# Hybrid decoder layer on one core: modulation weights loaded in 512-channel halves behind the input, their column sums formed on TensorE, first channel blocks without GpSimd

## Chip, cores, metric

The kernel runs on one core of a Trainium2 chip. The metric is the device time of one execution in microseconds (us): 1420.43 us is the median of three runs before the change (1417.43 to 1421.4). All numbers called a time are device time; the span of a profile is the part of it from the first to the last recorded instruction.

## What is computed

One layer of a conditioned hybrid decoder plus a final RMSNorm, for one sequence of 1024 tokens with 1024 channels. Only the start matters here:

```python
mod = silu(c) @ w_ada + b_ada        # (1, 1024) @ (1024, 6*1024)
sh1, sc1, gt1, sh2, sc2, gt2 = split(mod, 6)
h = rmsnorm(x, g_norm1) * (1 + sc1) + sh1
z = h @ w_in                         # (1024, 1024) @ (1024, 5128)
# then: gated convolution branch, mLSTM branch, merge, output projection,
# second norm with sc2/sh2, mixture of 32 experts, final RMSNorm
```

So the first product of `z` can't begin before the first rows of `sc1` and `sh1` (each 1024 long, from 8 MB of `w_ada` in all) are there for the channels that it contracts over. All inputs are float32. The products of the dense part are made of three products of rounded halves (`wh*hH + wl*hH + wh*hL`).

## The kernel before

Tokens and channels are cut in blocks of 128: 8 token blocks `xt[t]`, 8 channel blocks `xT[j]`. The program is emitted in a fixed order and each engine works through its own instructions in that order. Loads are issued on SP's queue.

**Loads (L1054 to L1075).** The first megabyte of `w_ada` (`ada_load(0)`) is issued ahead of `x`, then the 8 token blocks with the small vectors between them, then a second megabyte of `w_ada`, two half-megabyte pieces of `w_in` (`raw0`, `raw1`), and two more megabytes of `w_ada`. `run_start` then adds a third piece of `w_in` (`raw2`) and the last four megabytes. A megabyte of `w_ada` holds all 1024 rows by 256 columns: an even number is a quarter of the scale, an odd one a quarter of the shift.

**Start (`run_start`, L402).** A string lists the steps: `q` squares two token blocks on ScalarE, `r` takes their root mean square (VectorE, then GpSimd for the power), `s` scales a block, `t` transposes it with 8 products with the identity, `e` copies it back from PSUM (VectorE for blocks 0 to 2, ScalarE for the rest), `c` is `ada_chain`, `a` is `ada_cols`, `w` splits a piece of `w_in` into a rounded part `wh` (ScalarE) and the rest `wl` (GpSimd here), `v` transposes the small vectors.

**Columns of scale and shift.** `ada_chain(i)` multiplies and adds the 8 slices of a megabyte with the silu column on VectorE, 2 TENSOR_SCALAR and 6 SCALAR_TENSOR_TENSOR of 256 columns, and an addition from the third load on. `ada_cols(i)` sums over the partitions with products of 128x128 of the result by a column of ones on TensorE (8 products for loads 0 and 1, 4 for each later one).

**First products (`z_first`, L418).** Three pieces of 128 columns of `w_in` are multiplied in turn, a quarter of the contraction (2 channel blocks) at a time, so that the work can begin when the first quarter of scale and shift is known. Quarter `q` of piece `n` is the step `z` with the numbers n and q: 12 products of 128x512. `modulate(q)` forms scale and shift of 2 channel blocks, and for each block the modulated `xT[j]`, its rounded part `hH` and the rest `hL`. Blocks 0 and 6 are made on VectorE alone; the others on ScalarE (2 instructions) with the subtraction on GpSimd:

```python
"m0 w0 c2 c3 z00 a2 a3 z10 z20 m1 c4 c5 z01 a4 a5 z11 z21 m2 c6 c7 z02 a6 a7 z12 z22 m3 z03 z13 z23"
```

After it `run_late` (L457) gives up the space of `x` and `w_ada` and the rest of the dense part runs, with instructions of other parts filled in by budgets that are fixed when the program is emitted (`fill`).

Of the kernel before, what the change touches and what calls it, by code (L numbers as in the profile page):

```python
# [8 lines left out]
F32 = mybir.dt.float32  # L9
# [3 lines left out]
AF = mybir.ActivationFunctionType  # L13
OP = mybir.AluOpType
# [4 lines left out]
P = 128  # L19
T = 1024  # L20
D = 1024
NT = T // P
KT = D // P
# [19 lines left out]
def hybrid_layer_kernel(ctx: ExitStack, tc: tile.TileContext, x, c, w_ada, b_ada, g_norm1, w_in, b_if,  # L43
# [3 lines left out]
    nc = tc.nc  # L47
# [5 lines left out]
    V, S, G, PE = nc.vector, nc.scalar, nc.gpsimd, nc.tensor  # L53

    def tt(o, a, b, op, eng=V):
        return eng.tensor_tensor(out=o, in0=a, in1=b, op=op)  # L56

    def ts(o, a, s1, op0, s2=None, op1=None, eng=V):
        if op1 is None:
            return eng.tensor_scalar(out=o, in0=a, scalar1=s1, scalar2=None, op0=op0)  # L60
        return eng.tensor_scalar(out=o, in0=a, scalar1=s1, scalar2=s2, op0=op0, op1=op1)

    def stt(o, a, s, b, op0, op1):
        return V.scalar_tensor_tensor(out=o, in0=a, scalar=s, in1=b, op0=op0, op1=op1)  # L64

    def mm(o, l, r, start, stop):
        return PE.matmul(o, l, r, start=start, stop=stop)  # L67
# [15 lines left out]
    mps = ctx.enter_context(tc.tile_pool(name="mps", bufs=4, space=PSUM))  # L83
# [5 lines left out]
    hH = hTp.tile([P, KT, T], F32R, name="hH")  # L89
    hL = hTp.tile([P, KT, T], F32R, name="hL")  # L90
    st = tc.alloc_tile_pool(name="st", bufs=1, side="right")
    xall = st.tile([P, NT, D], F32, name="xall")
    xt = [xall[:, t, :] for t in range(NT)]
    xT = [xall[:, :, j * P:(j + 1) * P] for j in range(KT)]
    silc = cst.tile([P, KT], F32, name="silc")
# [3 lines left out]
    ones = cst.tile([P, P], F32, name="ones")  # L99
# [36 lines left out]
    def adab(vi, j, n):  # L136
        return vec[:, 64 + vi * KT + j:64 + vi * KT + j + n]
# [137 lines left out]
    W = Stream()  # L275
# [33 lines left out]
    araw = {}  # L309

    def ada_load(i):
        vi, q = (1, 0)[i % 2], i // 2
        araw[i] = st.tile([P, KT, 256], F32, tag="araw", bufs=8, name=f"araw{i}")
        nc.sync.dma_start(araw[i], ada_v[:, :, vi * D + q * 256:vi * D + (q + 1) * 256])

    def load_x(a, b):
        for t in range(a, b):
# [16 lines left out]

    def evacuate_x(t, ps):

        if t >= 3:
            S.copy(xt[t].rearrange("p (k n) -> p k n", n=P), ps)
        else:
            V.tensor_copy(xt[t].rearrange("p (k n) -> p k n", n=P), ps)  # L340

    pada = mps.tile([P, 512], F32, tag="m", name="pada")

    def ada_chain(i):

        a = araw[i]
        for k in range(4):
            for k0 in (0, 4):
                if k == 0:
                    ts(a[:, k0, :], a[:, k0, :], silc[:, k0:k0 + 1], OP.mult)  # L350
                else:
                    stt(a[:, k0, :], a[:, k0 + k, :], silc[:, k0 + k:k0 + k + 1], a[:, k0, :], OP.mult, OP.add)
        if i >= 2:
            tt(a[:, 0, :], a[:, 0, :], a[:, 4, :], OP.add)

    def ada_cols(i):

        vi, q = (1, 0)[i % 2], i // 2
        ks = (0,) if i >= 2 else (0, 4)
        for jj in range(2):  # L360
            o = pada[:, vi * KT + 2 * q + jj:vi * KT + 2 * q + jj + 1]
            for k0 in ks:
                mm(o, araw[i][:, k0, jj * P:(jj + 1) * P], ones[:, 0:1], k0 == 0, k0 == ks[-1])

    def tok(a):
        return a.rearrange("p (t n) -> p t n", n=P)

    def modulate(q):

        sl = slice(2 * q, 2 * q + 2)  # L370
        tt(A1[:, sl], pada[:, KT + 2 * q:KT + 2 * q + 2], adab(1, 2 * q, 2), OP.add)
        stt(A1[:, sl], A1[:, sl], 1.0, g1c[:, sl], OP.add, OP.mult)
        tt(S1[:, sl], pada[:, 2 * q:2 * q + 2], adab(0, 2 * q, 2), OP.add)
        for j in range(2 * q, 2 * q + 2):
            if j in (0, 6):
                ts(xT[j], xT[j], A1[:, j:j + 1], OP.mult, S1[:, j:j + 1], OP.add)
                V.tensor_copy(tok(hH[:, j, :]), xT[j])  # L377
            else:
                S.activation(xT[j], xT[j], AF.Identity, bias=S1[:, j:j + 1], scale=A1[:, j:j + 1])
                S.copy(tok(hH[:, j, :]), xT[j])  # L380
            tt(tok(hL[:, j, :]), xT[j], tok(hH[:, j, :].bitcast(F32)), OP.subtract, eng=V if j in (0, 6) else G)

    def load_third():

# [3 lines left out]
        nc.sync.dma_start(p["raw"], p["src"])  # L388
        W.nl += 1

    def split_on_pool(_):
        W.on_pool = 1
        W.split()

    def run_steps(steps, order_):

        for s_ in order_.split():
            steps[s_[0]](*(int(n) for n in s_[1:]))
# [1 line left out]
    psx = {}  # L400

    def run_start():  # L402
        ada_chain(0)
        run_steps({
            "q": lambda t: square_x(t, t + 2),
            "r": lambda t: rms_x(t, t + 2),
            "s": lambda t: ts(xt[t], xt[t], r1[:, t:t + 1], OP.mult),
            "t": lambda t: psx.update({t: transpose_x(t)}),
            "e": lambda t: evacuate_x(t, psx[t]),
            "c": ada_chain, "a": ada_cols, "l": ada_load, "w": split_on_pool,  # L410
            "x": lambda _: load_third(),
            "v": lambda _: vectors(),
        }, "q0 r0 s0 s1 a0 x0 l4 l5 l6 l7 t0 t1 q2 r2 e0 s2 s3 t2 q4 r4 e1 t3 s4 s5 q6 e2 t4 r6 e3 t5 s6 s7 t6 t7 "
           "c1 e4 e5 w0 w0 v0 e6 e7 a1")

    N_FIRST = 3

    def z_first(uses):  # L418

        ws = [W.take(), W.take()]  # L420
        ps2 = [zps.tile([P, 2, 512], F32, tag="z", name=f"z{i}") for i in range(2)]
        ps = [[a[:, 0, :], a[:, 1, :]] for a in ps2] + [[mps.tile([P, 512], F32, tag="m", name=f"z2_{hf}")
                                                          for hf in range(2)]]

        def third(_):
            split_on_pool(0)
            ws.append((W.pieces[2]["h"], W.pieces[2]["l"]))
            W.nu += 1

        def products(n, q):  # L430
            wh, wl = ws[n]
            for k in (2 * q, 2 * q + 1):
                for j, (a, b) in enumerate(((wh, hH), (wl, hH), (wh, hL))):
                    for hf in range(2):
                        mm(ps[n][hf], a[:, k, :], b[:, k, hf * 512:(hf + 1) * 512],
                           k == 0 and j == 0, k == KT - 1 and j == 2)

        run_steps({"m": modulate, "c": ada_chain, "a": ada_cols, "w": third, "z": products},
                  "m0 w0 c2 c3 z00 a2 a3 z10 z20 m1 c4 c5 z01 a4 a5 z11 z21 m2 c6 c7 z02 a6 a7 z12 z22 m3 z03 z13 z23")
        run_late()  # L440
        W.split()
        for i, use in enumerate(uses):
            use([ps2[i].rearrange("p a b -> p (a b)")] if i < 2 else ps[i])
        fill(3.0)
# [606 lines left out]
    n_dense = len(W.pieces)  # L1051


    ada_load(0)  # L1054

    vloads = []
    r0 = 0
# [9 lines left out]
    for t in range(NT):  # L1067
        load_x(t, t + 1)
        if t:
            for o, src in vloads[2 * t - 2:2 * t]:  # L1070
                nc.sync.dma_start(o, src)
    ada_load(1)
    W.prefetch()
    ada_load(2)
    ada_load(3)  # L1075
    run_start()
    for job in jobs:
        job()
# [1009 lines left out]
```

## Time and profile before

| | |
|---|---|
| median of 3 runs | 1420.43 us (1417.43 to 1421.4) |
| the profiled execution | 1411.8 us, span 1410.1 us |
| TensorE matmul busy | 1301.6 us (92%), 6619 instructions |
| VectorE busy | 985.6 us (70%) |
| ScalarE busy | 515.0 us (37%) |
| GpSimd busy | 318.4 us (23%) |
| first product of `z_first` starts | 37.21 us |
| the reader of its last result starts | 86.37 us |

The busy shares are means over very different stages: the dense part, in which TensorE is busy almost throughout, ends near 790 us; the experts behind it run with the transfers busy all the time. A busy TensorE is not one at its peak: the granted clock of a stretch stands beside its busy time.

### The profile page before, as it was taken

The page shows a single profiled execution, that of the slowest core. Times are in us where ns is not written, and L with a number is a line of the kernel's source. Part 1 is how long each engine was busy: PE and PEld are TensorE (multiplying, and loading weights), DVE is VectorE, ACT ScalarE, POOL GpSimd, SP SyncE. Part 2 cuts the span into 40 slices and gives each one's busy share as a digit, 9 for nine tenths or more (in the row PEclk, how much of TensorE's full clock was granted, in tenths as well). Part 3 has the DMA queues.
Part 4 walks back from the last instruction along what each step waited for, and adds up shares of the span by engine and source line. Part 5 has one row for each costly group of instructions (what it writes and reads, how often), then busy time and mean ns, then how long its engine had stood idle before and what let it go on. Part 6 is the DMA issues. An engine that isn't in the chain of part 4 may idle for free. (4 is left out here: it accounts for less than half of the span.)

```text
span 1410.1 us, 17680 instructions
## 1 busy us (share of the span) xinstructions
PE 1301.6 (92%) x6619; PEld 973.0 (69%) x6619; DVE 985.6 (70%) x1369; ACT 515.0 (37%) x685; POOL 318.4 (23%) x258
## 2 busy tenths in 40 slices
PE   4799888999999999999999599999898999999996
PEld 3677888879878888787888465656464656556743
DVE  6979998889976762556457786357576757666736
ACT  5232233323522224411232333225353444435613
POOL 2424355240421400105232101011011111111103
PEclk9799999999999999999999799999999999999998
DMA  9433433332454443354622559899999999999995
GB/s 287 134 120 135 139 132 134 116 107 78 149 172 134 145 132 111 140 183 149 199 91 75 183 224 382 325 376 410 419 411 408 406 398 405 381 404 389 396 366 228
DMA packets 121304, 337.50 MB, mean 239 GB/s; under 512 B 12532, under 2 KB 74272, under 8 KB 96384
## 3 DMA queue, kind: packets, MB, share of 16 engines
q1 hardware_dynamic: 106064, 290.81, 55.4%
q0 software_dynamic: 14672, 43.94, 8.2%
q10 hardware_dynamic: 480, 1.59, 0.3%
q8 instruction: 53, 0.87, 0.2%
q14 instruction: 35, 0.29, 0.1%
HBM read 303.37 MB, written 41.98 MB: 245 GB/s over the span
## 5 line engine op out<-in xcount | busy, mean ns | idle before, releaser
L56 DVE TENSOR_TENSOR wl<-big,wh 128x1024 fp32r<-128x1024 f32 x184 | 224.0, 1255 | 89.6 <-ACT wh L148 88.6
L148 ACT CAST wh<-big 128x1024 fp32r<-128x1024 f32 x184 | 185.6, 1049 | 152.8 <-DMA big<-in_w_e_gate_dram 80.4
L64 DVE SCALAR_TENSOR_TENSOR cacc<-u,vec,cacc 128x1024 f32<-128x1024 f32 x120 | 213.2, 1777 | 2.9
L67 PE MATMUL z<-hH,wh 128*128 128x512 f32 x512 | 167.0, 408 | 9.5 <-DVE hH L377 7.1
L67 PE MATMUL gu<-wh,tHLx 128*128 128x512 f32 x528 | 170.6, 404 | 1.6 <-ACT wh L148 1.0
L67 PE MATMUL z<-hL,wh 128*128 128x512 f32 x512 | 164.5, 403 | 0.0
L67 PE MATMUL z<-hH,wl 128*128 128x512 f32 x512 | 162.8, 399 | 0.0
L67 PE MATMUL gu<-big,tFx 128*64 128x512 f32 (+1 forms) x528 | 128.9, 625 | 0.0
L67 PEld LDWEIGHTS z<-hH,wh 128*128 128x128 f32 x512 | 97.0, 193 | 31.8 <-issue 8.2
L67 PEld LDWEIGHTS gu<-wh,tHLx 128*128 128x128 f32 x528 | 97.7, 191 | 27.5 <-ACT wh L148 6.5
L67 PEld LDWEIGHTS z<-hL,wh 128*128 128x128 f32 x512 | 98.3, 192 | 23.7
L67 PEld LDWEIGHTS z<-hH,wl 128*128 128x128 f32 x512 | 97.9, 191 | 24.2
L67 PE MATMUL gu<-wl,tHLx 128*128 128x512 f32 x264 | 106.7, 404 | 6.5 <-DVE wl L56 6.5
L1626 POOL DMA_INDIRECT y_d<-ye,idx x24 | 37.7, 1571 | 327.1 <-DVE ye L64 309.9
L56 DVE TENSOR_TENSOR wl<-raw,wh 128x1024 fp32r<-128x1024 f32 (+1 forms) x45 | 68.5, 1525 | 40.2 <-ACT wh L148 40.2
L67 PEld LDWEIGHTS gu<-big,tFx 128*64 128x64 f32 (+1 forms) x528 | 39.1, 144 | 72.3 <-issue 71.2
L56 POOL TENSOR_TENSOR acc<-acc,ar 128x1024 f32<-128x1024 f32 x24 | 72.0, 2998 | 61.0 <-ACT ar L572 52.1
L67 PE MATMUL zt<-wh,hH 128*128 128x256 f32 (+1 forms) x256 | 75.0, 293 | 2.5 <-DVE u L56 1.4
L67 PE MATMUL zt<-wl,hH 128*128 128x256 f32 (+1 forms) x256 | 73.9, 289 | 2.7 <-DVE wl L56 2.7
L67 PE MATMUL zt<-wh,hL 128*128 128x256 f32 (+1 forms) x256 | 74.1, 290 | 0.0
L67 PE MATMUL py<-wh,tHLh 128*128 128x512 f32 x256 | 72.8, 405 | 0.4 <-DVE tHLx L56 0.4
L67 PE MATMUL o<-woH,mHL 128*128 128x512 f32 x256 | 72.8, 400 | 0.0
(418 smaller groups left out, 2163.8 us busy)
## 6 DMA issues: line engine op xcount, KB each, us to landing
big<-in_w_e_gate_dram SPq DMA_DIRECT2D x64, 1024.0 KB
big<-in_w_e_up_dram SPq DMA_DIRECT2D x64, 1024.0 KB
big<-in_w_e_down_dram SPq DMA_DIRECT2D x64, 1024.0 KB
raw<-in_w_in_dram SPq DMA_DIRECT2D x38, 512.0 KB
ar<-in_w_ada_dram SPq DMA_DIRECT2D x16, 1024.0 KB
araw<-in_w_ada_dram SPq DMA_DIRECT2D x8, 1024.0 KB
y_d<-zero SPq DMA_DIRECT2D x16, 512.0 KB
xall<-in_x_dram SPq DMA_DIRECT2D x8, 512.0 KB
```

The source lines that it names most:

```text
L56: return eng.tensor_tensor(out=o, in0=a, in1=b, op=op)
L64: return V.scalar_tensor_tensor(out=o, in0=a, scalar=s, in1=b, op0=op0, op1=op1)
L67: return PE.matmul(o, l, r, start=start, stop=stop)
L148: S.copy(h, src)
L1626: G.indirect_dma_start(out=y_d[:, :], out_offset=bass.IndirectOffsetOnAxis(ap=idx[:, 1:2], axis=0), in_=src, in_offset=None, bounds_check= ...
```

## The change

Three things are altered, all within the first 90 us. The loads of `w_ada` are cut otherwise: a megabyte is now 512 columns of half of the rows, so that loads 0 to 3 give scale and shift of channels 0 to 511 and loads 4 to 7 the rest; they are issued behind all of `x` and behind the first piece of `w_in`. The sums of six of the eight loads are made on TensorE, 16 products of 128x128 by one silu column each; loads 4 and 6 still go over VectorE (4 instructions of 512 columns) and 4 products with ones. The modulation comes in two halves of 4 channel blocks; each block is scaled and shifted on VectorE, rounded on ScalarE and subtracted on VectorE. The three splits of `w_in` that ran on GpSimd run on VectorE, and the fourth token block comes back from PSUM by VectorE.

```diff
     def ada_load(i):
-        vi, q = (1, 0)[i % 2], i // 2
-        araw[i] = st.tile([P, KT, 256], F32, tag="araw", bufs=8, name=f"araw{i}")
-        nc.sync.dma_start(araw[i], ada_v[:, :, vi * D + q * 256:vi * D + (q + 1) * 256])
+
+        hq, vi, kk = i // 4, (1, 0)[i // 2 % 2], i % 2
+        araw[i] = st.tile([P, 4, 512], F32, tag="araw", bufs=8, name=f"araw{i}")
+        nc.sync.dma_start(araw[i], ada_v[:, 4 * kk:4 * kk + 4, vi * D + hq * 512:vi * D + (hq + 1) * 512])
...
-        if t >= 3:
+        if t >= 4:
             S.copy(xt[t].rearrange("p (k n) -> p k n", n=P), ps)
...
-    pada = mps.tile([P, 512], F32, tag="m", name="pada")
+    pada = [mps.tile([P, 512], F32, tag="m", name=f"pada{hq}") for hq in range(2)]
 
     def ada_chain(i):
 
-        a = araw[i]
-        for k in range(4):
-            for k0 in (0, 4):
-                if k == 0:
-                    ts(a[:, k0, :], a[:, k0, :], silc[:, k0:k0 + 1], OP.mult)
-                else:
-                    stt(a[:, k0, :], a[:, k0 + k, :], silc[:, k0 + k:k0 + k + 1], a[:, k0, :], OP.mult, OP.add)
-        if i >= 2:
-            tt(a[:, 0, :], a[:, 0, :], a[:, 4, :], OP.add)
+        a, c0 = araw[i], i % 2 * 4
+        ts(a[:, 0, :], a[:, 0, :], silc[:, c0:c0 + 1], OP.mult)
+        for k in range(1, 4):
+            stt(a[:, 0, :], a[:, k, :], silc[:, c0 + k:c0 + k + 1], a[:, 0, :], OP.mult, OP.add)
 
     def ada_cols(i):
 
-        vi, q = (1, 0)[i % 2], i // 2
-        ks = (0,) if i >= 2 else (0, 4)
-        for jj in range(2):
-            o = pada[:, vi * KT + 2 * q + jj:vi * KT + 2 * q + jj + 1]
-            for k0 in ks:
-                mm(o, araw[i][:, k0, jj * P:(jj + 1) * P], ones[:, 0:1], k0 == 0, k0 == ks[-1])
+        hq, vi, kk = i // 4, (1, 0)[i // 2 % 2], i % 2
+        for jj in range(4):
+            o = pada[hq][:, vi * 4 + jj:vi * 4 + jj + 1]
+            for k in range(1 if i in CHAINED else 4):
+                mm(o, araw[i][:, k, jj * P:(jj + 1) * P],
+                   ones[:, 0:1] if i in CHAINED else silc[:, 4 * kk + k:4 * kk + k + 1],
+                   i % 4 == 0 and jj == 0 and k == 0, i % 4 == 3 and jj == 3 and k == 3)
+
+    CHAINED = (4, 6)
...
-    def modulate(q):
-
-        sl = slice(2 * q, 2 * q + 2)
-        tt(A1[:, sl], pada[:, KT + 2 * q:KT + 2 * q + 2], adab(1, 2 * q, 2), OP.add)
+    def modulation(hq):
+
+        sl = slice(4 * hq, 4 * hq + 4)
+        tt(A1[:, sl], pada[hq][:, 4:8], adab(1, 4 * hq, 4), OP.add)
         stt(A1[:, sl], A1[:, sl], 1.0, g1c[:, sl], OP.add, OP.mult)
-        tt(S1[:, sl], pada[:, 2 * q:2 * q + 2], adab(0, 2 * q, 2), OP.add)
-        for j in range(2 * q, 2 * q + 2):
-            if j in (0, 6):
-                ts(xT[j], xT[j], A1[:, j:j + 1], OP.mult, S1[:, j:j + 1], OP.add)
-                V.tensor_copy(tok(hH[:, j, :]), xT[j])
-            else:
-                S.activation(xT[j], xT[j], AF.Identity, bias=S1[:, j:j + 1], scale=A1[:, j:j + 1])
-                S.copy(tok(hH[:, j, :]), xT[j])
-            tt(tok(hL[:, j, :]), xT[j], tok(hH[:, j, :].bitcast(F32)), OP.subtract, eng=V if j in (0, 6) else G)
+        tt(S1[:, sl], pada[hq][:, 0:4], adab(0, 4 * hq, 4), OP.add)
+
+    def modulate(j):
+
+        ts(xT[j], xT[j], A1[:, j:j + 1], OP.mult, S1[:, j:j + 1], OP.add)
+        S.copy(tok(hH[:, j, :]), xT[j])
+        tt(tok(hL[:, j, :]), xT[j], tok(hH[:, j, :].bitcast(F32)), OP.subtract)
...
     def run_start():
-        ada_chain(0)
...
-        }, "q0 r0 s0 s1 a0 x0 l4 l5 l6 l7 t0 t1 q2 r2 e0 s2 s3 t2 q4 r4 e1 t3 s4 s5 q6 e2 t4 r6 e3 t5 s6 s7 t6 t7 "
-           "c1 e4 e5 w0 w0 v0 e6 e7 a1")
+        }, "q0 r0 s0 s1 t0 t1 q2 r2 e0 s2 s3 t2 q4 r4 e1 t3 s4 s5 q6 e2 t4 r6 e3 t5 s6 s7 t6 e4 t7 e5 a0 x0 l4 l5 l6 l7 "
+           "e6 e7 v0 w0 a1 a2 a3")
...
-        run_steps({"m": modulate, "c": ada_chain, "a": ada_cols, "w": third, "z": products},
-                  "m0 w0 c2 c3 z00 a2 a3 z10 z20 m1 c4 c5 z01 a4 a5 z11 z21 m2 c6 c7 z02 a6 a7 z12 z22 m3 z03 z13 z23")
+        run_steps({"m": modulation, "h": modulate, "c": ada_chain, "a": ada_cols, "w": third, "z": products,
+                   "u": lambda _: ws.append(W.take())},
+                  "u0 m0 h0 h1 u1 z00 w0 h2 z10 h3 z20 c4 z01 z11 z21 a4 a5 c6 a6 a7 m1 h4 h5 z02 h6 z12 h7 z22 "
+                  "z03 z13 z23")
...
-    ada_load(0)
...
-    ada_load(1)
-    W.prefetch()
-    ada_load(2)
-    ada_load(3)
+    W.load()
+    for i in range(4):
+        ada_load(i)
+    W.load()
     run_start()
```

`split_on_pool`, which sent a subtraction to GpSimd, is gone; its callers now call `W.split()` itself. In the new string `m` forms scale and shift of a half, `h` modulates one channel block, and `u` takes a piece of `w_in` (for the second piece that is also its split).

## Rows read from the trace of the kernel before

**Rows 1.** The page's second part: TensorE's busy tenths and its granted clock, in 40 slices of 35 us.

```profile
PE   4799888999999999999999599999898999999996
...
PEclk9799999999999999999999799999999999999998
```

**Rows 2.** Stretches of 35 us, all engines: start and end, length, then busy time (and instructions) of PE, PEld, DVE, ACT and POOL, the granted clock of TensorE, the busy share of the DMA engines and GB/s.

```profile
105.00:140.00 35.00, 34.71 (x157) 27.91 (x156) 34.57 (x20) 9.30 (x9) 16.63 (x7) 1.00 0.36 127
...
175.00:210.00 35.00, 30.02 (x223) 29.44 (x222) 34.40 (x30) 14.67 (x17) 19.23 (x14) 0.90 0.37 120
...
1015.00:1050.00 35.00, 33.85 (x182) 22.71 (x179) 26.41 (x30) 19.13 (x23) 5.73 (x4) 1.00 1.01 416
```

**Rows 3.** The waits on TensorE from 30 to 90 us: engine, line, what was waited for, us in total, how often, the longest.

```profile
PE pada L67 <- DVE araw L56: 7.2, 4, 2.6
PE z L67 <- DVE hH L377: 7.1, 1, 7.1
```

**Rows 4.** The timeline at the first product of `z_first` and at the reader of its last one: start, us, engine, line, operation, and in brackets the idle time before it and what ended it.

```profile
37.21 1.19 PE L67 MATMUL z<-hH,wh 128*128 128x512 f32 x2 [7.14 <-DVE hH L377]
...
86.37 1.09 ACT L608 ACTIVATE sg<-z 128x512 f32<-128x512 f32 x2 [3.79 <-PE z L67]
```

**Rows 5.** Stretches of the start, columns as in rows 2.

```profile
24.00:26.50 2.50, 2.50 (x14) 2.50 (x13) 2.27 (x6) 1.09 (x2) 0.19 (x1) 0.50 1.17 297
...
27.30:29.00 1.70, 1.64 (x15) 1.40 (x14) 1.24 (x4) 1.68 (x3) 0.06 (x1) 1.00 1.11 331
...
30.10:33.70 3.60, 0.00 (x0) 0.00 (x0) 3.16 (x4) 3.54 (x4) 3.51 (x2) 1.00 1.09 345
...
34.00:40.00 6.00, 2.79 (x7) 2.24 (x8) 5.93 (x7) 1.15 (x2) 3.55 (x2) 0.50 1.12 333
...
44.60:47.20 2.60, 0.05 (x1) 0.00 (x0) 2.54 (x7) 0.00 (x0) 0.00 (x0) 0.50 1.09 347
...
61.50:64.60 3.10, 3.10 (x8) 2.43 (x8) 3.06 (x7) 3.04 (x4) 1.34 (x1) 0.50 0.00 0
...
92.00:120.00 28.00, 28.00 (x121) 22.50 (x120) 27.64 (x16) 7.50 (x8) 14.69 (x6) 1.00 0.40 132
```

**Rows 6.** The timeline where an engine stood until a load had landed: the first megabyte of `w_ada`, token blocks 4 and 7, and `raw2`; between the last two, the first product behind the last transpose.

```profile
9.22 0.61 DVE L60 TENSOR_SCALAR araw<-araw,silc 128x256 f32<-128x256 f32 x2 [6.32 <-DMA araw<-in_w_ada_dram]
...
16.57 1.06 ACT L323 ACTIVATE junk<-xall 128x1024 f32<-128x1024 f32 x1 [1.12 <-DMA xall<-in_x_dram]
...
22.02 1.06 ACT L323 ACTIVATE junk<-xall 128x1024 f32<-128x1024 f32 x1 [1.13 <-DMA xall<-in_x_dram]
...
28.90 0.27 PE L127 MATMUL pv<-ident,rows 128*128 128x128 f32 x1
...
37.66 1.04 ACT L148 CAST wh<-raw 128x1024 fp32r<-128x1024 f32 x1 [3.56 <-DMA raw<-in_w_in_dram]
```

**Rows 7.** SP's queue: its longest wait ahead of a load of `x`, and its issue of the last four loads of `w_ada`.

```profile
SPq L318 <- DMA araw<-in_w_ada_dram: 3.9, 1, 3.9
...
28.79 11.97 SPq L314 DMA_DIRECT2D araw<-in_w_ada_dram  x4
```

**Rows 8.** A stretch of 2 us in which the transfers ran short, columns as in rows 2.

```profile
12.00:14.00 2.00, 1.73 (x8) 1.64 (x8) 0.42 (x3) 1.89 (x4) 0.71 (x1) 1.00 0.49 161
```

**Rows 9.** Products of the column sums alone (tile `pada`), in two stretches; busy time of PE, PEld and DVE, then the granted clock.

```profile
11.80:13.80 2.00, 1.86 (x8) 1.78 (x8) 0.00 (x0) 1.00 0.49 165
...
29.00:30.10 1.10, 0.95 (x8) 0.97 (x8) 0.00 (x0) 1.00 1.10 350
```

**Rows 10.** Groups of instructions from 0 to 92 us: line, engine, operation, tiles, count, busy us and mean ns, idle time before them.

```profile
L64 DVE SCALAR_TENSOR_TENSOR araw<-araw,silc 128x256 f32<-128x256 f32 x48 | 21.8, 520 | 0.0
...
L60 DVE TENSOR_SCALAR araw<-araw,silc 128x256 f32<-128x256 f32 x16 | 9.2, 618 | 6.3 <-DMA araw<-in_w_ada_dram 6.3
...
L56 DVE TENSOR_TENSOR araw<-araw 128x256 f32<-128x256 f32 x6 | 6.8, 1128 | 0.2
...
L56 POOL TENSOR_TENSOR hL<-xall,hH 128x1024 fp32r<-128x1024 f32 x6 | 15.7, 2635 | 23.8 <-ACT hH L380 23.8
...
L56 POOL TENSOR_TENSOR wl<-raw,wh 128x1024 fp32r<-128x1024 f32 x3 | 7.4, 2472 | 7.0 <-ACT wh L148 7.0
...
L379 ACT ACTIVATE xall<-xall,S,A 128x1024 f32<-128x1024 f32 x6 | 7.4, 1242 | 25.2 <-DVE S L56 25.2
...
L380 ACT CAST hH<-xall 128x1024 fp32r<-128x1024 f32 x6 | 6.3, 1048 | 0.2
...
L56 DVE TENSOR_TENSOR hL<-xall,hH 128x1024 fp32r<-128x1024 f32 x2 | 2.5, 1226 | 0.1
...
L56 DVE TENSOR_TENSOR wl<-raw,wh 128x1024 fp32r<-128x1024 f32 x3 | 3.6, 1221 | 5.9 <-ACT wh L148 5.9
...
L340 DVE COPY xall<-xT 128x1024 f32<-128x1024 f32 x3 | 3.7, 1222 | 1.1 <-PE xT L332 1.1
```

**Rows 11.** The timeline, VectorE: modulation of one channel block beside no GpSimd work, and the column products of TensorE that it waited for.

```profile
71.91 0.60 PE L67 MATMUL pada<-ones,araw 128*128 128x1 f32 x4 [1.17 <-DVE araw L56]
...
73.01 0.81 DVE L61 TENSOR_SCALAR xall<-xall,A,S 128x1024 f32<-128x1024 f32 x1
```

**Rows 12.** The timeline, TensorE: two pairs of products behind one another in a stretch at half clock.

```profile
62.11 1.06 PE L67 MATMUL z<-hH,wh 128*128 128x512 f32 x2
...
62.97 1.06 PE L67 MATMUL z<-hH,wl 128*128 128x512 f32 x2
```

More of the change, by code (lines that the diff above doesn't have):

```diff
@@ L389, in load_third @@
         W.nl += 1
-    def split_on_pool(_):
-        W.on_pool = 1
-        W.split()
     def run_steps(steps, order_):
@@ L409, in run_start @@
             "e": lambda t: evacuate_x(t, psx[t]),
-            "c": ada_chain, "a": ada_cols, "l": ada_load, "w": split_on_pool,
+            "a": ada_cols, "l": ada_load, "w": lambda _: W.split(),
             "x": lambda _: load_third(),
             "v": lambda _: vectors(),
-        }, "q0 r0 s0 s1 a0 x0 l4 l5 l6 l7 t0 t1 q2 r2 e0 s2 s3 t2 q4 r4 e1 t3 s4 s5 q6 e2 t4 r6 e3 t5 s6 s7 t6 t7 "
-           "c1 e4 e5 w0 w0 v0 e6 e7 a1")
+        }, "q0 r0 s0 s1 t0 t1 q2 r2 e0 s2 s3 t2 q4 r4 e1 t3 s4 s5 q6 e2 t4 r6 e3 t5 s6 s7 t6 e4 t7 e5 a0 x0 l4 l5 l6 l7 "
+           "e6 e7 v0 w0 a1 a2 a3")
     N_FIRST = 3
     def z_first(uses):
-        ws = [W.take(), W.take()]
+        ws = []
         ps2 = [zps.tile([P, 2, 512], F32, tag="z", name=f"z{i}") for i in range(2)]
@@ L425, in third @@
         def third(_):
-            split_on_pool(0)
+            W.split()
             ws.append((W.pieces[2]["h"], W.pieces[2]["l"]))
```

## The prediction

> **What bounds the kernel now.** I read the 40 slices first. TensorE is busy for eight tenths or more from the third slice on, but for two slices where the experts begin, at nine tenths of the clock or more; the first two slices have 4 and 7 tenths, and in the second the granted clock is down to 7 [rows 1]. The change touches the first 90 us alone, so the question is by how much `z_first` ends earlier. What follows it takes a shift over: from 105 us TensorE and VectorE both run almost without a pause, later VectorE is the fuller of the two, and the experts are fed at 416 GB/s with the transfers always busy [rows 2]. All of these start from results of the dense part, in a fixed order; none has a date of its own.
>
> Next the waits and the timeline of the start. `z_first` runs from 37.2 us to 86.3 us, 49.1 us [rows 4]. Its 144 products need 144 x 0.231 = 33.3 us at full clock (28.0 us for 121 [rows 5]), so 15.8 us go elsewhere: 7.2 us to columns that wait for VectorE [rows 3], the rest to column products and half clock. VectorE is what feeds it: the chains over `w_ada` take 37.8 us there, and the additions, 1.13 us in the mean, are drawn out beside GpSimd's subtractions of 2.6 us [rows 10]. After each idle stretch TensorE runs at clock 0.50: from 34 to 40 us, and from 61.5 to 64.6 us [rows 5], where a pair of products takes 0.86 us, 0.43 each [rows 12].
>
> **The loads.** Before, a megabyte of `w_ada` lies ahead of `x`, SP waits 3.9 us for it before it can issue another token block [rows 7], and the transfers then fall to 161 GB/s [rows 8]. Block 7 lands at 22.0 us [rows 6]. Moving the megabyte behind `x` takes 1.05 MB at 345 GB/s [rows 5], 3.0 us, off that; of the wait I take 2.5 us, between 0 and 3.9, because the small vectors still stand between the blocks. Block 7 then lands at 16.5 us (15.1 to 19.0).
>
> Now all of scale and shift for half of the channels must land, not a quarter. From block 7 to the fourth `w_ada` load there are one piece of `w_in` and four megabytes, 4.72 MB, the same bytes that took 15.6 us from block 7 to `raw2` before [rows 6]. The piece at 297 GB/s takes 1.8 us; `w_ada` I price at 345 GB/s, 12.2 us, since the rows of 2 KB are nearest to the rows of 1 KB that ran at that rate [rows 5]: 14.0 us. Ends: 15.6 us, and 11.3 us at the 416 GB/s of the experts [rows 2]. The fourth load lands at 30.5 us (26.4 to 34.6). Issues on SP cost nothing: `raw2` and the last four loads are issued behind and their 12 us of issuing [rows 7] lie beside the transfers; they land some 16 us later, well ahead of their use after 54 us. [...]
>
> **Columns on TensorE.** 104 products in place of 40. Eight took 0.95 us in one stretch and 1.86 us in another [rows 9], so 16 cost 1.9 us or 3.7 us. `a1` to `a3` make TensorE wait for transfers; behind them stand only the products that need them anyway. Block 7 to the last transpose took 28.9 - 22.0 = 6.9 us [rows 6], so `a0` can begin at 23.4 us; at full clock TensorE keeps up (23.4 + 0.4 for the vectors + 4 x 1.9 = 31.4 us), and the fourth load ends last: 30.5 + 0.1 + 1.9 = 32.5 us. From column products to modulation took 0.5 us (71.91 + 0.60 to 73.01 [rows 11]): modulation begins at 33.0 us. Five PSUM tiles now share four buffers, but `z20` needs the first only after modulation has read it: nothing. Block 3's copy back on VectorE, 1.22 us [rows 10], lies ahead of block 7's last steps, and the first piece's subtraction, moved to VectorE, beside the column products: nothing.
>
> **First half.** A channel block costs 0.81 us on VectorE [rows 11], 1.05 us on ScalarE and 1.23 us on VectorE again [rows 10], with handovers (0.05 each, an estimate) 3.2 us; the subtraction waits for ScalarE and the next block's scaling is queued behind it, so blocks don't overlap. The first product starts at 33.0 + 0.81 + 1.05 + 0.15 = 35.0 us, 2.2 us earlier. Four blocks and two weight subtractions of 1.22 us [rows 10] put the last subtraction at 33.0 + 12.8 + 2.4 = 48.2 us; TensorE needs 11.1 us for its 48 products by then and waits; `z01` ends at 48.7 us. `z11` and `z21`: 24 x 0.231 = 5.6 us, to 54.3 us.
>
> **Second half.** Columns 4 to 7 are 40 products, 4.8 us, to 59.1 us. The chains `c4` and `c6` are 8 instructions in place of 70; even at twice the mean of 0.5 to 0.6 us [rows 10] they end at 52.5 and 57 us, when `a4` is due at 54.3 and `a6` at 56.7: nothing. Modulation starts at 59.6 us, `z02` at 61.6 us, and ends with block 5's subtraction at 66.0 + 0.5 = 66.5 us; blocks 6 and 7 hide behind the 60 products left, 13.9 us. End: 80.4 us. GpSimd loses 23.1 us of work and ScalarE six instructions of 1.24 us [rows 10]; nobody waits for either beyond what is counted.
>
> **The clock.** TensorE is idle or underused before 35 us and before 61.6 us. A restart costs 8 products or more at 0.43 instead of 0.23 us [rows 5, 12]; the waits for VectorE, some 2 us spare in each half, cover one of the two. I take 1.6 us for the other and 0.3 us for stragglers (0 to 5): 82.3 us instead of 86.3, **4.0 us saved**. The profiled execution took 1411.8 us with a span of 1410.1; it would take 1407.8. It lies 8.6 us under the median of the three runs, which are runs of the same program, so I take the same 4.0 us off the median: 1416.4 us.
>
> **Rivals.** About 0.3%, 4.3 us, can be told from no change.
>
> 1. *More*, 0.10: `w_ada` in rows of 2 KB comes at 416 GB/s, block 7 at 15.1 us and no restart is uncovered. That saves 4 to 9 us: 1411.8 us at best. Against it: TensorE's own columns then bind at about 31 us.
> 2. *The loads come no sooner*, 0.12: both upper ends, 34.6 us for the fourth load, 4.1 us later: the gain is gone, 1420.5 us. For it: the 15.6 us are measured; against it: the 161 GB/s show idle transfers.
> 3. *Columns at half clock*, 0.08: 23.4 + 0.4 + 4 x 3.7 = 38.6 us instead of 32.5; end 88.4 us, 1422.5 us, inside the bound. Against it: with nothing but transposes running, the clock rose from 0.50 to 1.00 [rows 5]. [...] No row shows a long run of one-column products.
> 4. *Slower*, 0.10: half clock stays from the columns through the first half. Blocks reach TensorE singly, so it is never busy for long there; 48 products at 0.43 are 20.6 us from 41.1 us on, so `z01` ends at 61.7 instead of 48.7 us, and the end at 93.4 us: 1427.5 us. It decides from the point where `z01` ends 10 us late. For it: each idle stretch before was followed by half clock [rows 5]. Against it: the pieces `z10` and `z20` are ready by then and keep TensorE busy.
> 5. *Given back later*, 0.04: VectorE is full from 92 us [rows 5], and some wait behind absorbs it: 1420.4 us.
>
> **The numbers.** The forecast has 0.56; its own range, 2 to 7 us saved, is 1413.4 to 1418.4 us, with 0.32 beyond the bound and 0.24 within. Faster: 0.32 + 0.10 = 0.42. No change: 0.24 + 0.12 + 0.08 + 0.04 = 0.48. Slower: 0.10. The range reaches from rival 1 to rival 3, 1411.8 to 1422.8 us; left out are rival 4 and the tails, under 0.2.
>
> **What the changed profile would show.** Block 7's square at 16.5 us, the last of `a3` at 32.5, the first product at 35.0, `z01` over at 48.7, 40 column products in one run up to 59 at full clock, a pause of 2.5 us, the reader of the last result at 82.3 us, and from there the same stretches 4 us earlier. No GpSimd instruction of 2.6 us before 80 us, and VectorE's subtractions all near 1.22 us. A first product after 37 us would make the loads or the columns the fault; a granted clock of 0.50 through most of 35 to 50 us would make rival 4 right.

## The result, and the profile after

The changed kernel takes 1435.93 us (median of 4 runs, 1433.2 to 1441.54), the kernel before 1418.93 us beside it (4 runs): the ratio is 1.0147, with a 95% interval of 1.012 to 1.0174. The forecast was 1416.4 us, in a range of 1411.8 to 1422.8. The time is 17 us longer by the medians, 21 us by the ratio, where 4 us less was expected.

The profiled execution took 1436.94 us with a span of 1435.1. The first thing to find is where the two kernels part. The same stretch as the second of [rows 2], put 20.6 us later, is this in the kernel after (columns as there):

```profile
195.60:230.60 35.00, 30.03 (x223) 29.44 (x222) 34.40 (x31) 14.69 (x17) 19.23 (x14) 0.90 0.38 123
```

All five engines have the same busy times as at 175 us before, to 0.02 us, with the same counts but for one instruction of VectorE (31 for 30). So by then the program does just what it did, 20.6 us late; what went wrong lies ahead of it. The rows that answer to [rows 4], the first product of `z_first` and the reader of its last one:

```profile
54.18 1.22 PE L67 MATMUL z<-hH,wh 128*128 128x512 f32 x2 [2.50 <-ACT hH L377]
...
106.96 1.09 ACT L602 ACTIVATE sg<-z 128x512 f32<-128x512 f32 x2 [3.84 <-PE z L67]
```

The first product is 17.0 us later than before (37.21) and 19.2 us later than forecast (35.0). The reader is 20.6 us later than before and 24.7 us later than forecast. Most of the loss is therefore ahead of the first product. Who is late there is in VectorE's longest wait; its timeline at the two modulations:

```profile
51.72 0.16 DVE L56 TENSOR_TENSOR A<-pada,vec 128x4 f32<-128x4 f32 x1 [18.73 <-PE pada L67]
...
52.19 0.81 DVE L61 TENSOR_SCALAR xall<-xall,A,S 128x1024 f32<-128x1024 f32 x1
```

VectorE stands 18.7 us for the column sums. That wait replaces the ones of [rows 3], in which TensorE stood for VectorE. And TensorE isn't waiting for a load in that time. Its own timeline, from the last transposes to the first product, and then the two long loads of the second half:

```profile
27.12 3.76 PE L67 MATMUL pada<-silc,araw 128*128 128x1 f32 x32
...
31.19 20.48 PE L67 MATMUL pada<-silc,araw 128*128 128x1 f32 x96
...
74.04 3.71 PE L67 MATMUL pada<-silc,araw 128*128 128x1 f32 x32
...
78.74 6.96 PE L67 MATMUL pada<-silc,araw 128*128 128x1 f32 x32
```

Two things are to be read here. First the counts: a load was said to be 16 products, and its row has 32 instructions; three loads have 96. The groups of instructions by line, over the first 110 us, have the total:

```profile
L67 PE MATMUL pada<-silc,araw 128*128 128x1 f32 x192 | 34.9, 318 | 0.0
L67 PE MATMUL pada<-ones,araw 128*128 128x1 f32 x16 | 2.2, 259 | 0.0
```

That is 208 instructions where the prediction counted 104 products. Then the pace: 3.76 us for the first 32 is 0.118 us each, 20.48 us for the next 96 is 0.213 each. The second half repeats it: 3.71 us for 32, then 6.96 us for 32. Beside them the granted clock, by stretches (columns as in [rows 2]; 1.00 is full clock and 0.50 half of it, and the 0.93 and 0.80 are of stretches that have both); the last four lie in the run of `a4` to `a7`, which begins at 73.2 us:

```profile
22.00:27.00 5.00, 5.00 (x24) 5.00 (x25) 0.00 (x0) 2.03 (x2) 0.00 (x0) 0.50 1.05 387
27.00:31.00 4.00, 4.00 (x36) 4.00 (x35) 0.00 (x0) 1.96 (x2) 0.00 (x0) 0.93 1.12 340
31.00:34.00 3.00, 3.00 (x16) 3.00 (x16) 1.55 (x2) 0.00 (x0) 0.00 (x0) 0.50 1.13 333
34.00:38.00 4.00, 4.00 (x20) 4.00 (x20) 0.00 (x0) 0.00 (x0) 0.00 (x0) 0.50 1.05 388
...
46.00:50.00 4.00, 4.00 (x20) 4.00 (x21) 0.00 (x0) 0.00 (x0) 0.00 (x0) 0.50 0.00 0
...
74.00:77.60 3.60, 3.60 (x34) 3.60 (x34) 0.00 (x0) 0.00 (x0) 0.00 (x0) 1.00 0.00 0
77.60:78.70 1.10, 1.10 (x10) 1.10 (x10) 0.00 (x0) 0.00 (x0) 0.00 (x0) 0.80 0.00 0
78.70:82.00 3.30, 3.30 (x17) 3.30 (x17) 0.00 (x0) 0.00 (x0) 0.00 (x0) 0.50 0.02 5
82.00:85.70 3.70, 3.70 (x18) 3.62 (x17) 0.00 (x0) 0.00 (x0) 0.00 (x0) 0.50 0.00 0
```

TensorE's busy time fills every one of these stretches, so there is no idle time that could explain a fall of the clock, as there was before or in each half-clock stretch of [rows 5] (1.36, 7.14, 2.01 and 1.40 us, ending at 23.4, 37.2, 43.9 and 59.8 us). Yet the clock goes from 1.00 to 0.50 at 30.5 us and again at 78.3, each time with nothing but column products running, and from 31 us it stays at 0.50 as long as they run. Nor do loads hold the columns up: TensorE never pauses for one, and from 46 to 50 us, and again from 74, next to nothing is moved. The page's second part shows it at once, beside [rows 1]: in the first two slices TensorE is busier than before, 6 and 9 tenths for 4 and 7, and in the second its clock is lower, 6 for 7. (The first slice's clocks, 7 and 9, can't be set side by side: the trace of the kernel before has no record of the clock ahead of 20.2 us, and that of the kernel after none ahead of 13.4 us, and 1.00 is printed there.)

```profile
PE   6999988999999999999999689999999999899996
...
PEclk7689998999999999999999889999999999999998
```

### The profile page after: what moved, and what is told of

Same layout as the page of the kernel before. It is cut to its first block, busy times and chain, and to the rows that moved or that the text cites. A ratio compares the mean times of both kernels' runs of the same rounds, so it can differ in the third digit from the quotient of the medians.

```text
span 1435.1 us, 17939 instructions
## 1 busy us (share of the span) xinstructions
PE 1337.5 (93%) x6787; PEld 1007.8 (70%) x6787; DVE 963.7 (67%) x1315; ACT 508.9 (35%) x680; POOL 294.2 (21%) x249
## 5 line engine op out<-in xcount | busy, mean ns | idle before, releaser
L67 PEld LDWEIGHTS z<-hH,wl 128*128 128x128 f32 x512 | 97.6, 191 | 24.4 <-DVE wl L56 0.4
L1619 POOL DMA_INDIRECT y_d<-ye,idx x24 | 37.7, 1571 | 333.0 <-DVE ye L64 312.8
```

The costliest lines, as they stand in the source:

```text
L1619: G.indirect_dma_start(out=y_d[:, :], out_offset=bass.IndirectOffsetOnAxis(ap=idx[:, 1:2], axis=0), in_=src, in_offset=None, bounds_check= ...
```

## Experiments

Theory A: the columns' own time is the loss, by two faults of the sum, the count (32 instructions a load) and the half clock under one-column products. Rival B: the loads of half of the channels are what the start waits for, and TensorE is busy only because it has the time. Rival C: the third part, blocks without GpSimd, is slower. Rival D: the order of the loads is worth nothing. The table has every run; "rest" is the profiled execution's time less that of the reader. The quoted expectations use other letters: theory C is what the run was expected to show (A, in the first three), rival L is B and rival K is C. Each ratio is to runs of the kernel before in the same sitting, with a median of 1414.12 us beside the first four experiments that were run (half of the products, 64 equal columns, all loads over VectorE, blocks without GpSimd) and 1416.39 us beside the other three.

| kernel | first product, us | reader, us | profiled execution, us | rest, us | ratio to before, 95% |
|---|---|---|---|---|---|
| before | 37.21 | 86.37 | 1411.8 | 1325.4 | |
| after | 54.18 | 106.96 | 1436.94 | 1330.0 | 1.0147, 1.012 to 1.0174 |
| half of the products | 37.73 | 86.12 | 1415.33 | 1329.2 | 0.999, 0.9967 to 1.0013 |
| 64 equal columns | 41.70 | 92.50 | 1419.93 | 1327.4 | 1.005, 1.0028 to 1.0072 |
| all loads over VectorE | 42.15 | 89.15 | 1418.54 | 1329.4 | 1.0008, 0.9985 to 1.0031 |
| before, blocks without GpSimd | 35.73 | 93.40 | 1423.41 | 1330.0 | 1.0038, 1.001 to 1.0066 |
| quarters behind `x` | 33.05 | 77.50 | 1404.47 | 1327.0 | 0.9937, 0.9913 to 0.9961 |
| before, loads behind `x` | 33.89 | 86.69 | 1416.87 | 1330.2 | 0.9988, 0.9968 to 1.0008 |
| 64 columns, blocks in pairs | 43.49 | 94.44 | 1422.14 | 1327.7 | 1.0047, 1.0027 to 1.0067 |

The rest lies between 1325 and 1330 us in all nine, while the reader moves over 29 us; the 4.6 us between the rests of before and after are inside that spread. What is won or lost by `z_first` stays won or lost, and each kernel can be judged by its reader.

**Half of the products.** The kernel after, with products for two of the four slices of each load that doesn't go over VectorE.

```diff
-            for k in range(1 if i in CHAINED else 4):
+            for k in range(1 if i in CHAINED else 2):
...
-                   i % 4 == 0 and jj == 0 and k == 0, i % 4 == 3 and jj == 3 and k == 3)
+                   i % 4 == 0 and jj == 0 and k == 0, i % 4 == 3 and jj == 3 and k == 1)
```

> Of the 16 column products of each load that isn't chained, only those of 2 of 4 slices are made: half of these sums are left out, so scale and shift lack those parts. Theory C (the column products on TensorE are what got dear: each is two instructions, 32 a load, and they run at half clock): 64 instructions fewer ahead of the first half at 0.12 (the first load) to 0.21 us (the others) take 12 us off the first product, from 54.2 to about 42 us, and with 32 fewer ahead of the second half the last result is read about 17 us earlier, near 90 us; time near 1419 us. Rival L (the loads of scale and shift for half of the channels land too late): first product still at 54 us, 1436 us. Rival K (blocks that pass from VectorE to ScalarE and back without GpSimd): 54 us and 1436 us, nothing of that is touched.

The first product came at 37.73 us, 16.4 us sooner than in the kernel after, the reader at 86.12, 20.8 us sooner, with all loads as they were. That is more than A's number, for a reason of A's own kind: the first 48 instructions ran at full clock but for the very last, and only the last 16 were slow.

```profile
24.43 1.84 PE L67 MATMUL pada<-silc,araw 128*128 128x1 f32 x16
...
26.39 3.75 PE L67 MATMUL pada<-silc,araw 128*128 128x1 f32 x32
31.65 3.57 PE L67 MATMUL pada<-silc,araw 128*128 128x1 f32 x16 [1.51 <-DMA araw<-in_w_ada_dram]
```

The clock fell at 30.0 us, before the pause that the last line shows. `a0` also began at 24.43 us instead of 27.12, since the transposes ahead of it ran at full clock for longer in this execution. Rival B is out for the first product: the same bytes were there for products to begin at 37.7 us. Here the loads do show, as a wait of 1.5 us ahead of the last 16.

**64 equal columns.** The silu column is read as 64 equal columns, so that each product writes 64 equal columns of PSUM; the modulation reads one of them. Number and weights of the products stay.

```diff
-            o = pada[hq][:, vi * 4 + jj:vi * 4 + jj + 1]
+            o = pada[hq][:, (vi * 4 + jj) * 64:(vi * 4 + jj + 1) * 64]
...
-                   ones[:, 0:1] if i in CHAINED else silc[:, 4 * kk + k:4 * kk + k + 1],
+                   (ones[:, 0:1] if i in CHAINED else silc[:, 4 * kk + k:4 * kk + k + 1]).broadcast_to([P, 64]),
...
```

> The same column products, each with 64 equal columns streamed instead of one: as many instructions, more columns. Theory C1 (the granted clock follows the columns that stream through TensorE, not its busy share): the clock stays at 1.00 through the columns, an instruction takes 0.12 to 0.14 us instead of 0.21, the 96 instructions of loads 1 to 3 take 12 to 13.5 us instead of 20.5, the first product starts at 46 to 47 us, and the last load's 7.0 us become 4: the last result is read some 10 us earlier, 1426 us. Rival C2 (a busy TensorE at half clock has another cause, and wider products only add work): still 0.50, first product at 54 us or later, 1436 us or more. Under L or K: no change.

This is the experiment that separates the clock from the count. The timeline of TensorE in it:

```profile
24.62 3.68 PE L67 MATMUL pada<-silc,araw 128*128 128x64 f32 x32
28.37 10.83 PE L67 MATMUL pada<-silc,araw 128*128 128x64 f32 x96
```

The same 96 instructions, each over 64 times as many columns, take 10.83 us instead of 20.48; 12 to 13.5 were expected. The stretch that was at 0.50 in the kernel after is at 1.00 here:

```profile
30.00:34.00 4.00, 4.00 (x38) 4.00 (x38) 0.12 (x1) 0.00 (x0) 0.00 (x0) 1.00 1.13 335
34.00:38.00 4.00, 4.00 (x38) 4.00 (x38) 0.00 (x0) 0.00 (x0) 0.00 (x0) 1.00 1.05 387
```

In this execution `a0` began at full clock and 2.5 us sooner than in the kernel after, so one might put the difference down to that. The last experiment, below, answers it. The reader is at 92.50 us, 14.5 us sooner than in the kernel after, of which the earlier `a0` is 2.5, and still 6.1 us later than before: half clock was the larger part of the loss, not all of it. At 1.005 the kernel at full clock through the columns is still slower than before. The 104 instructions that the sum left out take 11.8 us at 0.113 each, more than the 6.1 us; that they alone are what is left wasn't measured.

**All loads over VectorE.** The kernel after with four VectorE instructions of 512 columns ahead of each load's columns, and 4 products with ones instead of 16 with silu.

```diff
...
-    CHAINED = (4, 6)
+    CHAINED = tuple(range(8))
...
-            ... s6 s7 t6 e4 t7 e5 a0 x0 l4 l5 l6 l7 e6 e7 v0 w0 a1 a2 a3"
+            ... s6 s7 t6 e4 t7 e5 c0 a0 x0 l4 l5 l6 l7 e6 e7 v0 c1 w0 a1 c2 a2 c3 a3"
...
-                  "u0 m0 h0 h1 u1 z00 w0 h2 z10 h3 z20 c4 z01 z11 z21 a4 a5 c6 a6 a7 m1 ...
+                  "u0 m0 h0 h1 u1 z00 w0 h2 z10 h3 z20 c4 z01 c5 z11 c6 z21 c7 a4 a5 a6 a7 m1 ...
```

> The column part alone undone: all eight loads go over VectorE (4 instructions of 512 columns each) and then 4 products with ones on TensorE, loads and modulation stay as in the changed kernel. Theory C: 8 column instructions a load instead of 32; the last chain ends near 34 us, first product at 37 to 38 us, but VectorE now carries 11 us of chains in each half, so the last result is read at 86 us give or take 2: 1418 us, as before the change. Rival L: first product still after 50 us. Rival K: first product near 37 us, the last result still read after 95 us, 1428 us or more.

The total is as expected and the way to it isn't. The first product came at 42.15 us: VectorE's second chain stood behind the copy of the small vectors, which waited until 27.9 us, and the columns of each later load of the first half took 1.86 us or 1.87 for 8 instructions, at half clock, with TensorE waiting for VectorE ahead of each. So the work fits on VectorE without GpSimd beside it, 2.8 us a load, and the start is 12.0 us sooner than in the kernel after, but halves in this order bring nothing over the kernel before: the reader, expected at 86 us give or take 2, is at 89.15.

**The third part alone.** The kernel before with every channel block scaled on VectorE, rounded on ScalarE and subtracted on VectorE, and the splits of `w_in` on VectorE.

```diff
-            if j in (0, 6):
-                ts(xT[j], xT[j], A1[:, j:j + 1], OP.mult, S1[:, j:j + 1], OP.add)
-                V.tensor_copy(tok(hH[:, j, :]), xT[j])
-            else:
-                S.activation(xT[j], xT[j], AF.Identity, bias=S1[:, j:j + 1], scale=A1[:, j:j + 1])
-                S.copy(tok(hH[:, j, :]), xT[j])
-            tt(tok(hL[:, j, :]), xT[j], tok(hH[:, j, :].bitcast(F32)), OP.subtract, eng=V if j in (0, 6) else G)
+            ts(xT[j], xT[j], A1[:, j:j + 1], OP.mult, S1[:, j:j + 1], OP.add)
+            S.copy(tok(hH[:, j, :]), xT[j])
+            tt(tok(hL[:, j, :]), xT[j], tok(hH[:, j, :].bitcast(F32)), OP.subtract)
...
-        W.on_pool = 1
```

> The kernel before with the third part alone: scaling on VectorE, rounding on ScalarE, subtraction on VectorE for every channel block, no GpSimd in the splits. Theory C: VectorE is no longer drawn out by GpSimd, so the first product comes at 33 us instead of 37, but it waits for ScalarE in each block and carries 14 us a quarter; the last result is read at 86 to 87 us, 1419 us, no change within 4 us. Rival K: this part alone makes the kernel slower by 10 us or more. L: no change.

A miss: the reader was expected at 86 to 87 us and is 7.0 us later than before. VectorE's own instructions are fast (each of the six additions of the chains takes 0.42 us; the mean of 1.13 before [rows 10] is of four with 0.42 or 0.43 and two with 2.54 and 2.53, at 51.6 and 63.8 us, while GpSimd subtracted), and, as the timeline of one block shows, it stands still while ScalarE rounds:

```profile
33.78 0.81 DVE L61 TENSOR_SCALAR xall<-xall,A,S 128x1024 f32<-128x1024 f32 x1
35.70 1.23 DVE L56 TENSOR_TENSOR hL<-xall,hH 128x1024 fp32r<-128x1024 f32 x1 [1.11 <-ACT hH L376]
```

With four modulations and 16 chains that stand in between, these waits lie in the way of the next chain: TensorE's wait for VectorE's column sums, from 30 us to the end of `z_first`, is 12.0 us here against 7.2 [rows 3]. So rival C is real at the quarter arrangement, and the third part has a price by itself that the sum didn't have.

**The load order alone.** The kernel before with its first megabyte of `w_ada` issued behind `x`, and its chain and columns put behind the transposes.

```diff
-        ada_chain(0)
...
-        ... "q0 r0 s0 s1 a0 x0 ... t6 t7 c1 e4 e5 w0 w0 v0 e6 e7 a1"
+        ... "q0 r0 s0 s1 x0 ... t6 t7 c0 c1 e4 e5 w0 w0 v0 e6 e7 a0 a1"
...
-    ada_load(0)
-
...
+    ada_load(0)
```

> The kernel before with the load order alone changed: the first megabyte of the modulation weights behind x, its sums behind the transposes; quarters, VectorE chains and GpSimd as before. Theory C: the loads are not the fault; block 7 lands at 18 us instead of 22, the first product comes 0 to 3 us earlier than 37.2 us and the last result is read at 83 to 86 us: 1411 to 1414 us, same to slightly faster. Rival L (moving the modulation weights behind x is what delays the start): first product after 40 us, 1418 us or more.

The first product is 3.3 us sooner and the reader, expected at 83 to 86 us, is where it was, at 86.69. Rival D is right for this arrangement: VectorE's chains, drawn out as they were before (two of the six additions take 2.53 and 2.54 us, the other four 0.42, as all six do in the kernel without GpSimd's subtractions), space the quarters, whose modulations begin at 29.5, 47.0, 59.2 and 71.3 us. An earlier start that the bounding engine doesn't share is gone by the end of `z_first`.

**Quarters behind `x`.** Put together from the parts that bring something: the loads behind `x`, quarters as before, one tile with 256 columns of scale and 256 of shift, so that VectorE takes both in one instruction of 512 columns; products with ones only; no GpSimd; blocks scaled and rounded on ScalarE (the very first scaled on VectorE) and subtracted on VectorE, so that the two blocks of a quarter overlap. The small vectors are transposed earlier, and the first two loads go ahead of the first piece of `w_in`.

```diff
...
-        araw[i] = st.tile([P, KT, 256], F32, tag="araw", bufs=8, name=f"araw{i}")
-        nc.sync.dma_start(araw[i], ada_v[:, :, vi * D + q * 256:vi * D + (q + 1) * 256])
+        araw[i] = st.tile([P, 4, 512], F32, tag="araw", bufs=8, name=f"araw{i}")
+        for vi in range(2):
+            nc.sync.dma_start(araw[i][:, :, vi * 256:(vi + 1) * 256],
+                              ada_v[:, 4 * kk:4 * kk + 4, vi * D + q * 256:vi * D + (q + 1) * 256])
...
+        acc = araw[2 * q][:, 0, :]
+        for k in range(a, b):
+            src = araw[2 * q + k // 4][:, k % 4, :]
...
+                  "u0 m0 T0 u1 C0 A1 C1 S0 c102 S1 z00 z01 c124 w0 c148 z10 z11 z20 a1 z21 "
+                  "m1 A2 C2 A3 C3 c203 S2 c234 S3 z02 z03 c248 z12 z13 a2 z22 z23 "
...
```

(`T` scales a block on VectorE, `A` on ScalarE, `C` rounds on ScalarE, `S` subtracts on VectorE; `c` with three numbers is a part of a quarter's chain.)

> A new arrangement from what the first four runs showed: scale and shift load by quarters again (two channel blocks at a time) but behind x, a quarter of scale and a quarter of shift side by side so that one VectorE instruction of 512 columns covers both; all sums on VectorE (8 instructions a quarter), 8 column instructions a quarter on TensorE; scaling and rounding of the blocks on ScalarE except the first, subtractions on VectorE, nothing on GpSimd. Theory C (TensorE's column products were the cost, and no GpSimd beside VectorE is worth something once ScalarE takes the scaling): first product at 32 to 33 us, a quarter every 9 to 10 us, the last result read at 75 to 78 us instead of 86, and all of it arrives at the end: 8 to 11 us under before, 1403 to 1406 us where before is 1414. Rival G (given back later: VectorE is full from 92 us on, so a start that ends early is absorbed): under 3 us saved.

The first product is at 33.05 us and the reader at 77.50, 8.9 us sooner than before. The ratio of 0.9937 is 8.9 us of 1416.39 (median 1406.99 us), so this kernel is faster than the kernel before, clear of the noise, by 0.6%, as was expected. Which of its parts earns this no run separates. Where it wins is in TensorE's clock and waits; two stretches of it, and behind them the same two of the kernel before:

```profile
40.00:60.00 20.00, 17.99 (x79) 12.85 (x78) 15.18 (x25) 8.97 (x8) 0.00 (x0) 1.00 0.45 137
60.00:78.00 18.00, 17.57 (x75) 12.90 (x74) 10.48 (x14) 6.97 (x8) 0.12 (x1) 1.00 0.32 98
...
40.00:60.00 20.00, 14.02 (x57) 11.22 (x56) 18.43 (x36) 4.48 (x4) 6.83 (x3) 0.81 0.50 155
60.00:78.00 18.00, 16.83 (x72) 13.73 (x72) 14.46 (x27) 6.78 (x6) 7.93 (x3) 0.91 0.00 1
```

From 40 us on the clock is 1.00, where before it was 0.81 and 0.91; TensorE is idle for 2.4 us of the 38, where before it was for 7.2.

**64 columns, blocks in pairs.** The kernel with 64 equal columns, with every second block scaled on ScalarE so that two blocks overlap.

```diff
...
-                  "u0 m0 h0 h1 u1 z00 w0 h2 z10 h3 z20 c4 z01 z11 z21 a4 a5 c6 a6 a7 m1 h4 h5 z02 h6 z12 h7 z22 "
+                  "u0 m0 T0 A1 C0 C1 S0 u1 S1 T2 A3 C2 C3 z00 w0 S2 z10 S3 z20 c4 z01 z11 z21 a4 a5 c6 a6 a7 "
+                  "m1 T4 A5 C4 C5 S4 T6 S5 A7 C6 C7 z02 S6 z12 S7 z22 z03 z13 z23"
```

> The column products with 64 equal columns as in the second run, and every second channel block scaled on ScalarE so that two blocks overlap. Theory C: what the second run still lacked against the kernel before (7 us) is the count of column instructions and the passing of single blocks between VectorE and ScalarE; with pairs the stretch from the first product to the last result read shrinks from 50.8 to about 46 us, read at 87 to 88 us, 1415 to 1417 us, the same as before. If passing between the engines costs nothing (the wait is hidden by TensorE's own work): 92 us and 1421 us as in the second run.

A miss: 1421.52 us, and the way from the first product to the reader is 50.9 us, as in the kernel with single blocks (50.8). In the first half the casts of `w_in` stand behind the blocks on ScalarE and VectorE waits up to 3.0 us for them. In the second half the blocks are ready sooner, but TensorE meets them at half clock (0.58 from 73 to 77 us, 0.57 from 77 to 81), and from its first product there to the reader it takes 19.1 us instead of 19.5.

But its start answers what was left open above. Here the transposes ran at half clock up to 26 us, as in the kernel after, and the columns began right behind them:

```profile
22.00:26.00 4.00, 4.00 (x21) 4.00 (x20) 0.00 (x0) 2.02 (x2) 0.00 (x0) 0.52 1.05 387
26.00:30.00 4.00, 4.00 (x39) 4.00 (x38) 0.00 (x0) 1.96 (x2) 0.00 (x0) 1.00 1.08 361
30.00:34.00 4.00, 4.00 (x39) 4.00 (x37) 1.55 (x2) 0.00 (x0) 0.00 (x0) 1.00 1.15 324
34.00:38.00 4.00, 4.00 (x39) 4.00 (x37) 0.00 (x0) 0.00 (x0) 0.00 (x0) 1.00 1.04 386
```

The first 32 instructions take 3.68 us, the next 96 take 10.83 us again, at 1.00 throughout. With much the same stretch ahead of them, only the width of the products differs. That the clock falls here under one-column products and not under the same products with 64 columns, and that this costs the kernel after 9.7 us in the first half (20.48 - 10.83; 9.2 against the pace of its own first 32), is shown.

## Why the prediction was wrong

**The step that failed** is "Columns on TensorE": "104 products in place of 40 ... so 16 cost 1.9 us or 3.7 us ... at full clock TensorE keeps up". It failed twice.

*The count was mis-sized by two.* The 104 was counted in the code and the 40 in the trace, and these are different units. In the code of before, `ada_cols` makes 2 x 2 products for the first two loads each and 2 for each of the other six, 20 in all; the trace has 40, and [rows 9] show 8 for a load with 4; so the "8 products for loads 0 and 1, 4 for each later one" of the description are instructions. A float32 product by a column is two instructions in both traces. The change has 104 products and 208 instructions, and 16 products cost 3.76 us at full clock, not 1.9. That could have been read from the rows and the code before.

*The clock.* Half clock was a rival, not the forecast. It stood at 0.08 because the transposes of [rows 5] ran up to 1.00, and it had the columns at half clock from their start, carried over from the transposes; measured, they start at 1.00 and lose it while they run. No row of before showed a long run of one-column products, as the text said, and transposes move 128 columns each. That rival's price, 3.7 us for 16, is what they cost at full clock; its end of 88.4 us was 18.6 us short. The busy column of the profile after is full from 22 to 50 us and the clock fell at 30.5 us all the same, 8.5 us after TensorE had last stood idle.

The end of `a3` was forecast at 32.5 us and measured at 51.7 (31.19 + 20.48). Term by term:

| | us |
|---|---|
| `a0` begins at 27.12, not 23.4; 64 instructions at 0.1175 and 0.3 for the vectors would end at 34.95 | 2.5 |
| 128 instructions, not 64: 64 x 0.1175 | 7.5 |
| 96 of them at 0.213 instead of 0.1175 | 9.2 |
| sum | 19.2 |

From there to the reader the forecast was 49.8 us, and it took 55.3. The columns of the second half are the whole of it: 12.5 us (73.24 to 85.70) in place of 4.8, 7.7 more, of which 80 instructions at full clock would be 4.6 and half clock the rest. The other stretches came to 2.2 us less, 1.9 of them what had been set aside for the clock.

The other steps, each by its own row:

- *Loads.* Block 7's square began at 18.0 us (forecast 16.5, range to 19.0). The loads as such were in time: with half of the products, the columns waited only 1.5 us for the last of the four, to 31.65 us (forecast 30.5). Near enough as priced.
- *`a0` from 23.4 us.* 3.7 us off: 1.5 by block 7, 2.2 behind it. The last 24 transposes ran at 0.50 throughout and took 5.29 us, while [rows 5] had 1.00 near their end; in two other executions of the same code up to there they reached full clock, took 4.17 and 4.49 us, and `a0` began at 24.4 and 24.6 us. So 0.8 to 1.1 us of the 2.2 are the clock of these 24, and the rest lies ahead of them: they began 4.0 us after block 7's square, and in the other two 2.1 and 2.9 us after it.
- *Columns to modulation, and a block*: 51.7 to 52.19 to the first product at 54.18 us, 2.5 us as forecast. VectorE's scaling took 0.81 us, its subtractions 1.23, blocks followed at 3.1 us. Right. The 0.05 us for each handover was the author's estimate and no run shows it; the first block has 0.09 us from VectorE to ScalarE (53.00 to 53.09) and 0.03 back (54.13 to 54.16).
- *First half of the products*: 54.18 to 73.24 us is 19.1 us, forecast 19.3. *From the columns to the reader*: 85.70 to 106.96 is 21.3 us, as the working had it without its allowance for the clock.
- *"All of these start from results of the dense part"*: right. The shift of 20.6 us passes on to the stretch at 195 us unchanged, and the rest of the execution is 1325 to 1330 us in all kernels.
- *The slower rival*, half clock from the columns through the first half: half right. It gave 41.1 us for the first product and 61.7 for the end of `z01`; the columns were slow, but the products behind them were at 0.68 from 54 to 60 us and at 1.00 from 60 to 70: half clock ended 3.6 us after the wide products began. Its ground, that each idle stretch before was followed by half clock, is not quite what the trace has: behind the idle 1.17 us of [rows 11] the clock of the kernel before is 1.00 from 71.9 to 76 us.

What the experiments add is that the other parts are no gain in these orders of work: loads behind `x` bring 3.3 us at the first product and none at the end, blocks without GpSimd, one behind the other, cost 7.0 us in quarters, and the whole change with its sums over VectorE comes out even. Whether the change would have saved the 4.0 us with its columns as cheap as forecast wasn't measured.

Open: why the transposes ran at full clock in some executions and at half in others; what it is in a one-column product that lets the clock fall; and whether the loss of 9.2 us would be smaller with, say, 8 columns. The first of [rows 9], 8 instructions in 1.86 us beside a printed clock of 1.00, is no exception to the paces above: 8 such instructions take 1.86 us beside 0.50 where all loads go over VectorE, and that 1.00 is printed ahead of the trace's first record of the clock.

## What to carry to other kernels

Count an added instruction in the unit in which its duration was taken: find the same line of code in the trace and divide the instructions there by the calls in the code, before multiplying. A long run of one-column products on TensorE should be priced at half clock as well as at full (0.213 and 0.1175 us an instruction here), even where nothing idles, unless a row shows such a run keeping full clock. And the clock of a stretch is checked against the pace of its instructions, since a profile can print 1.00 where it has no record, as that of the kernel before has none ahead of 20.2 us. Last, a part of a change that starts the work sooner is worth what reaches the engine that spaces the stage behind it, which the reader of the stage's last result shows better than its first instruction.

## What the runs showed of the hardware that was not expected

The granted clock fell from 1.00 to 0.50 while TensorE was busy without a pause, at 30.5 and at 78.3 us, under products of 128x128 weights by one column; with 64 equal columns the same products kept 1.00 through 128 instructions in two executions. At full clock an instruction took 0.113 us with 64 columns and 0.1175 with one, so the 63 further columns cost nothing that can be seen, and at half clock one with a single column took 0.213 us. A float32 product by a column stands in the trace as two instructions (20 products and 40 instructions before, 104 and 208 after), a product with both operands in fp32r as one (144 of each in `z_first`).
